# Reordering the last piece's second products, moving half of a gate, and a tile for one weight sum, in a two-layer backbone on one core

## The chip, the core and the metric

The kernel runs on one core of a Trainium2 chip. Its engines are named as in the profile: PE is TensorE (matrix products), PEld its weight loads, DVE is VectorE, ACT is ScalarE, POOL is GpSimd, SP is SyncE, whose queue issues the DMAs. The metric is the device time of one execution in microseconds (us). Before the change it is 2649.41 us, the median of 3 runs (2645.65 to 2652.79).

## What is computed

Two layers work on 512 latent and 128 context tokens of width 1024 in fp32. Each layer is a gated feed-forward block, a token mixer, and a second feed-forward block, so there are four feed-forward blocks in all. The change touches these alone:

```
def swiglu(h, wi, wo):                    # wi: 1024 x 5632, wo: 2816 x 1024
    a, b = jnp.split(h @ wi, 2, axis=-1)
    return (jax.nn.silu(a) * b) @ wo

def trunk_layer(x, mod, ...):
    h = mod_norm(x, norm_g[0], mod, 0)
    x = x + 0.5 * mod[..., 2, :] * swiglu(h, ffn1_wi, ffn1_wo)
    ...                                   # token mixing
    h = mod_norm(x, norm_g[2], mod, 2)
    x = x + 0.5 * mod[..., 8, :] * swiglu(h, ffn2_wi, ffn2_wo)
```

## The kernel before

**Number format.** Every operand of a product is cut in two: a high part (a copy rounded to the matmul's format, on ACT, L265 for weights) and a low part (the rest, a subtraction, on POOL L266 for weights and on DVE L816 for the gated activations). A product is three matmuls into one PSUM sum: high weight by high activation (L449), high weight by low activation (L450), low weight by high activation (L451).

**First products.** The 2816 hidden columns are 22 blocks j of 128. For one j the two halves a and b of the gate come from seven products per block (a 2x2 Strassen-Winograd scheme over the two column groups and the two token halves of 320), in the order S2, S5, A22, A11, S1, S6, S7. Each is twelve matmuls at L773. Their operands on the activation side are B11, B22, X4, X3, X1, X6, X7 (in the profile the names B, X, P, Q). Results go into four PSUM banks, C and E in one tile, D and A in another. After each product DVE or ACT takes its bank: ACT b L831 (S2), DVE b L838 (S5), DVE a L856 (A22), ACT a L846 and DVE b L847 (A11, S1, S6), DVE a L842 and the silu at ACT a L843 (S7). The next product into the same tile waits for such a reader: A22 for L831, S1 for L856.

**The weight sums.** S2, S5, S1 use sums of raw weights, formed on DVE at L124: two in-place differences on the raw buffers (`raw<-raw`, S6 and S7) and one sum into a working tile, `sq` for S2 and S1, `acc` for S5. ACT and POOL then read the sum. `pump` does as many of these conversions as slots allow, after each step; they run about one block j ahead of the products.

**The gate.** `finish`, called in step S7, multiplies the silu'd a by b in two halves of 320 tokens: half 0 reads b in SBUF (`b<-a,b`), half 1 reads bank D (`b<-a,ps`), both at L807. Later `end` makes the high part (ACT av L815) and the low part (DVE av L816). This pair is a "piece".

**Second products.** The j are taken in groups of 4, 2, 4, 4, 4, 4. After a group its n pieces are multiplied by the rows of wo: for each of 8 output slices d, for both token halves g, n pieces of three matmuls, 192 matmuls for n = 4 (`down_part`; `down` for the last group, one g after the other, with the next norm woven in). The rule `late` lets the first `ahead` slices d take all pieces but the last, and only then the last piece of those d, since it is ready latest. Then DVE adds the result to x at L663, which frees the PSUM tile; there are four such tiles. In the first two feed-forward blocks to run, some slices are followed by a burst of small matmuls for the modulation parameters (L376), a copy on ACT (L381) and a transpose on PE (L390).

**Order.** Every engine runs its instructions in the order in which the program writes them; nothing reorders them later.

Of the kernel before, what the change touches and what calls it, by code (L numbers as in the profile page):

```python
# [24 lines left out]
KD = D // 128  # L25
# [59 lines left out]
class Kernel:  # L85
# [26 lines left out]
    def ffn_convs(self, f, u0):  # L112
# [3 lines left out]
        out = []  # L116
# [11 lines left out]
        for j in first:  # L128
            b = ab(j)[1]
# [28 lines left out]
        def s1(r):  # L158
            s7(r)
            s6(r)  # L160
            into(self.nb["sq"][:, :512], q(r[0], 0), q(r[1], 1))

        j0, ud = 0, u0 + 2 * NFF
        for name, j in ((name, j) for j in first for name in ("S1", "S7", "S6")):
# [8 lines left out]
        for gi, gn in enumerate(FFG):  # L173
            for j in range(max(j0, FIRST), j0 + gn):
                a, b = ab(j)
                conv("S2", j, (a, b), lambda r: self.nb["sq"][:, :512], s2)
                conv("S5", j, (a, b), lambda r: self.nb["acc"][:, :512], s5)
                conv("A22", j, (a, b), lambda r: q(r[1], 1))
                conv("A11", j, (a, b), lambda r: q(r[0], 0))
                conv("S1", j, (a, b), lambda r: self.nb["sq"][:, :512], s1)  # L180
                conv("S6", j, (a, b), lambda r: q(r[1], 0), frees=(b,))
                conv("S7", j, (a,), lambda r: q(r[0], 1), frees=(a,))
            for i in range(gn * KD // 8):
                for h in range(2):
                    conv("D", (gi, 2 * i + h), (ud,), lambda r, h=h: q(r[0], h), frees=(ud,) if h else ())
                ud += 1
            j0 += gn
# [256 lines left out]
        return self.modv[l][:, 8 * s + d, cond : cond + 1]  # L444


    def mm3(self, out, w, x, start, stop):
        mm = self.nc.tensor.matmul
        mm(out, w[0], x[0], start=start, stop=False)  # L449
        mm(out, w[0], x[1], start=False, stop=False)  # L450
        mm(out, w[1], x[0], start=False, stop=stop)  # L451

    def rsqrt(self, v, y, a):

# [224 lines left out]
    @staticmethod  # L679
    def late(n, ahead):  # L680


        out = [(d, range(n - 1)) for d in range(ahead)] + [(d, (n - 1,)) for d in range(ahead)]
        return out + [(d, range(n)) for d in range(ahead, KD)]

    def down(self, l, s, pieces, nxt, get, free, ahead, rest=None):

# [5 lines left out]
            self.wcap = 8  # L693
        for g in (1, 0):
            pss = {}
            for d, ks in self.late(n, ahead) if g else [(d, range(n)) for d in range(KD)]:
                self.now += 1
                w = get(d)
                if d not in pss:
                    pss[d] = self.psum()  # L700
                ps = pss[d]
                for k in ks:
                    self.mm3(self.part(ps, g), w(k), pieces[k](g), k == 0, k == n - 1)
                if ks[-1] != n - 1:
                    continue
                if g == d == 0:
                    self.ada_rest()
# [33 lines left out]
    def down_part(self, l, s, pieces, get, free=None, ds=range(KD), ahead=0):  # L741
        n = len(pieces)
        pss = {}
        for d, ks in self.late(n, ahead) if ahead else [(d, range(n)) for d in ds]:
            self.now += 2
            w = get(d)
            if d not in pss:
                pss[d] = self.psum()
            ps = pss[d]
            for g in (1, 0):  # L750
                for k in ks:
                    self.mm3(self.part(ps, g), w(k), pieces[k](g), k == 0, k == n - 1)
            if ks[-1] != n - 1:
                continue
            if free:
                free(d)
            m = 512 - self.geo.n[0]
            flat = ps[:].rearrange("p a b -> p (a b)")[:, m : m + NT]
            self.x_add(l, s, d, flat, ((0, NLAT, 0), (NLAT, NT, 1)), 0)
            self.ada_rest()  # L760
            if free:
                self.pump()
                if d in ADA_AT or (l, 8 * s + KD - 1) not in self.modset:
                    self.ada_tick()
# [14 lines left out]
    def ffn(self, l, s, gate, nxt):  # L779
# [28 lines left out]

        def finish(p, pair):

            gated(p, 0)
            gated(p, 1)
            hi, lo = pair
            b = p["b"]
            ends.append(lambda: nc.scalar.activation(hi, b, AF.Copy))  # L815
            ends.append(lambda: tt(lo, b, hi.bitcast(F32), op=sub))  # L816
# [170 lines left out]
        for gi, gn in enumerate(FFG):  # L987
            pairs = first() if gi == 0 else None
            for j in range(FIRST if gi == 0 else j0, j0 + gn):
                p = new(j)  # L990
                if s and j == NFF - 2:
                    self.ada_stop = True
                banks(p, "CE")
                banks(p, "DA")
                step(p, "S2")
                end(1)
                step(p, "S5")
                end()
                step(p, "A22")
                self.ada_tick()  # L1000
                step(p, "A11")
                step(p, "S1")
                if l == s == 0:
                    self.ada_tick()
                step(p, "S6")
                if pairs is None:
                    pairs = av(gn)
                step(p, "S7", lambda: finish(p, pairs[j - j0]))
# [12 lines left out]
                    self.block_free((f, "D", (gi, d // per)))  # L1021

            if gi < len(FFG) - 1:
                self.down_part(l, gate, pieces, get, free, ahead=2 if n == 4 else 3)
            else:
                if s == 0:
                    self.less_raws((3,))
                else:
# [4 lines left out]
                    self.ada_rest()  # L1033
                    if nxt is not None:
                        self.more_raws((3, 4, 5, 6))
                self.down(l, gate, pieces, nxt, get, free, 2)
                for v in vslots:
                    self.unslot(v)
            j0 += gn
# [962 lines left out]
```

## Time and profile before

| what | value |
|---|---|
| median of 3 runs | 2649.41 us (2645.65 to 2652.79) |
| the profiled execution's own time | 2643.27 us |
| its span, first to last instruction | 2641.2 us |
| PE busy | 2399.8 us, 91% of the span, 17790 matmuls |
| POOL busy | 1551.3 us, 59% |
| DVE busy | 1685.8 us, 64% |
| mean granted TensorE clock | 0.964 of full speed |

A busy PE is not a PE at its peak, as matmuls are pipelined; what counts is how closely one follows another. Idle time of the other engines costs nothing unless PE waits at its end.

### The profile page before, as it was taken

To read this page: it belongs to the slowest core of one execution; us is meant where nothing else is said; L and a number is where in the kernel's file an instruction comes from. 1 tells how busy PE (TensorE), PEld (TensorE's weight loads), DVE (VectorE), ACT (ScalarE), POOL (GpSimd) and SP (SyncE) were. 2 spreads that over 40 slices of the span, in tenths; PEclk is the share of its full clock that TensorE was granted. 3 is DMA by queue.
4 is the path that set the end of the run, shared out by engine and by line. 5 is a ranking of instruction groups with operands and counts; after the bars stand their busy time and mean duration, and the time that the engine had idled before them with its cause. 6 is when DMAs were issued, how large, how long until landed. Compare 5 with 4: busy or idle time off the path is not lost. (4 is left out here: it accounts for less than half of the span.)

```text
span 2641.2 us, 45318 instructions
## 1 busy us (share of the span) xinstructions
PE 2399.8 (91%) x17790; PEld 2330.7 (88%) x17790; DVE 1685.8 (64%) x2902; ACT 1045.4 (40%) x2242; POOL 1551.3 (59%) x1489
## 2 busy tenths in 40 slices
PE   4699999989889899999997999999889898999999
PEld 4699999979889899999987899999889788999999
DVE  5556566567676966555568666556766768566654
ACT  4333233333664533233244332334437644233332
POOL 2655566653366765465556665666434668576553
PEclk7899999989999899999998999999899998999999
DMA  7455422221103224555232221223111133122121
GB/s 269 147 205 208 153 88 80 80 93 55 35 33 104 88 97 174 211 222 198 83 100 71 93 72 65 80 80 123 37 52 43 49 104 112 64 82 87 56 80 48
DMA packets 80484, 272.31 MB, mean 103 GB/s; under 512 B 9233, under 2 KB 15121, under 8 KB 80273
## 3 DMA queue, kind: packets, MB, share of 16 engines
q1 hardware_dynamic: 79408, 269.33, 30.0%
q8 instruction: 140, 2.29, 0.4%
q14 instruction: 72, 0.58, 0.1%
q10 hardware_dynamic: 864, 0.10, 0.0%
HBM read 265.73 MB, written 3.67 MB: 102 GB/s over the span
## 5 line engine op out<-in xcount | busy, mean ns | idle before, releaser
L266 POOL TENSOR_TENSOR wt<-raw,wt 128x512 fp32r<-128x512 f32 (+1 forms) x562 | 875.0, 1575 | 496.9 <-ACT wt L265 493.8
L450 PE MATMUL ps<-av,wt 128*128 128x320 f32 (+2 forms) x1536 | 482.9, 314 | 24.1 <-DVE av L816 24.1
L449 PE MATMUL ps<-av,wt 128*128 128x320 f32 (+2 forms) x1536 | 484.1, 315 | 11.5 <-ACT av L815 11.5
L265 ACT ACTIVATE wt<-raw 128x512 fp32r<-128x512 f32 (+1 forms) x562 | 349.7, 658 | 345.8 <-PE ps L451 120.9
L451 PE MATMUL ps<-av,wt 128*128 128x320 f32 (+2 forms) x1536 | 479.8, 312 | 0.0
L663 DVE SCALAR_TENSOR_TENSOR x<-ps,modv,x 128x512 f32<-128x512 f32 (+3 forms) x496 | 233.3, 513 | 341.9 <-PE ps L451 341.5
L773 PE MATMUL ps<-X,wt 128*128 128x320 f32 x2112 | 355.0, 318 | 48.8 <-DVE a L856 20.3
L773 PEld LDWEIGHTS ps<-X,wt 128*128 128x128 f32 x2112 | 322.9, 193 | 63.1 <-DVE a L856 26.7
L266 POOL TENSOR_TENSOR wt<-sq,wt 128x512 fp32r<-128x512 f32 x144 | 204.3, 1419 | 252.4 <-ACT wt L265 214.4
L773 PE MATMUL ps<-B,wt 128*128 128x320 f32 x2112 | 335.8, 316 | 17.5 <-ACT wt L265 8.0
L773 PEld LDWEIGHTS ps<-B,wt 128*128 128x128 f32 x2112 | 323.2, 193 | 18.7 <-ACT wt L265 8.2
L450 PEld LDWEIGHTS ps<-av,wt 128*128 128x128 f32 x1536 | 294.0, 191 | 30.4 <-DVE av L816 30.3
L773 PE MATMUL ps<-P,wt 128*128 128x320 f32 x1760 | 295.2, 316 | 18.1 <-DVE a L856 11.2
L449 PEld LDWEIGHTS ps<-av,wt 128*128 128x128 f32 x1536 | 293.9, 191 | 15.2 <-ACT av L815 12.5
L451 PEld LDWEIGHTS ps<-av,wt 128*128 128x128 f32 x1536 | 294.0, 191 | 0.0
L773 PEld LDWEIGHTS ps<-P,wt 128*128 128x128 f32 x1760 | 270.3, 192 | 24.9 <-issue 15.2
L847 DVE TENSOR_TENSOR b<-ps,b 128x320 f32<-128x320 f32 x240 | 117.4, 490 | 197.0 <-PE ps L773 135.7
L773 PE MATMUL ps<-Q,wt 128*128 128x320 f32 x1408 | 237.2, 311 | 4.8 <-DVE b L847 4.8
L773 PEld LDWEIGHTS ps<-Q,wt 128*128 128x128 f32 x1408 | 215.6, 190 | 6.0 <-DVE b L847 5.6
L124 DVE TENSOR_TENSOR raw<-raw 128x512 f32<-128x512 f32 x163 | 185.2, 1170 | 8.9 <-DMA raw<-in_w 6.6
L124 DVE TENSOR_TENSOR sq<-raw 128x512 f32<-128x512 f32 x125 | 160.1, 1281 | 29.7 <-POOL wt L266 25.1
L265 ACT ACTIVATE wt<-sq 128x512 fp32r<-128x512 f32 x144 | 90.9, 631 | 221.7 <-DVE sq L124 137.0
(269 smaller groups left out, 3948.4 us busy)
## 6 DMA issues: line engine op xcount, KB each, us to landing
raw<-in_w SPq DMA_DIRECT2D x311, 512.0 KB, 3.6
ada<-in_adat SPq DMA_DIRECT2D x40, 1024.0 KB, 7.5
ada<-in_adat SPq DMA_DIRECT2D x64, 512.0 KB, 6.5
scraw<-in_w SPq DMA_DIRECT2D x33, 512.0 KB, 4.0
x<-in_xt SPq DMA_DIRECT2D x2, 1280.0 KB, 7.8
out_yt<-x SPq DMA_DIRECT2D x16, 160.0 KB, 1.8
dft<-in_dft SPq DMA_DIRECT2D x4, 512.0 KB, 4.1
kqv<-in_inv SPq DMA_DIRECT2D x4, 336.0 KB, 3.9
```

Of the source, the lines that this page charges most:

```text
L124: eng.tensor_tensor(o, x, y, op=op)
L265: nc.scalar.activation(hi, src, AF.Copy)
L266: nc.gpsimd.tensor_tensor(lo, src, hi.bitcast(F32), op=ALU.subtract)
L449: mm(out, w[0], x[0], start=start, stop=False)
L450: mm(out, w[0], x[1], start=False, stop=False)
L451: mm(out, w[1], x[0], start=False, stop=stop)
L663: self.nc.vector.scalar_tensor_tensor(out=self.x[:, d, c0:c1], in0=ps[:, c0 - o : c1 - o], scalar=self.mod(l, s, d, cond), in1=self.x[:, d ...
L773: mm(out, w[:, k * 128 : k * 128 + 128], v[:, k * 320 : k * 320 + 320], start=start and i == k == 0, stop=i == 2 and k == 3, skip_group_ch ...
L847: tt(p["b"][:, half[0]], bank, p["b"][:, half[0]], op=sub if p["neg"] else add)
```

## The change

Three edits. (1) `mm3` can issue only the high-activation matmuls of a product (part 0) or only the low-activation one (part 1). `late` then takes, for the first `ahead` slices, the last piece's high parts for all of them and after that its low parts for all of them; `ahead` is 3 everywhere, where it was 2 for groups of four and in `down`. (2) Half 0 of the gate is issued in step S6 rather than in step S7 (for the first four j it stays). (3) S1's sum goes to the tile `t` instead of `sq`.

```
-            into(self.nb["sq"][:, :512], q(r[0], 0), q(r[1], 1))
+            into(self.nb["t"][:, :512], q(r[0], 0), q(r[1], 1))
...
-                conv("S1", j, (a, b), lambda r: self.nb["sq"][:, :512], s1)
+                conv("S1", j, (a, b), lambda r: self.nb["t"][:, :512], s1)
...
-    def mm3(self, out, w, x, start, stop):
+    def mm3(self, out, w, x, start, stop, part=None):
+
         mm = self.nc.tensor.matmul
-        mm(out, w[0], x[0], start=start, stop=False)
-        mm(out, w[0], x[1], start=False, stop=False)
-        mm(out, w[1], x[0], start=False, stop=stop)
+        if part != 1:
+            mm(out, w[0], x[0], start=start, stop=False)
+        if part != 0:
+            mm(out, w[0], x[1], start=False, stop=part == 1 and stop)
+        if part != 1:
+            mm(out, w[1], x[0], start=False, stop=part is None and stop)
...
-        out = [(d, range(n - 1)) for d in range(ahead)] + [(d, (n - 1,)) for d in range(ahead)]
-        return out + [(d, range(n)) for d in range(ahead, KD)]
+        out = [(d, range(n - 1), None, False) for d in range(ahead)]
+        out += [(d, (n - 1,), i, i == 1) for i in range(2) for d in range(ahead)]
+        return out + [(d, range(n), None, True) for d in range(ahead, KD)]
...
-                if ks[-1] != n - 1:
+                if not all_d:
                     continue
...
-            gated(p, 0)
+            if p["early"]:
+                gated(p, 0)
             gated(p, 1)
...
-                step(p, "S6")
+                step(p, "S6", lambda: gated(p, 0))
...
-                self.down_part(l, gate, pieces, get, free, ahead=2 if n == 4 else 3)
+                self.down_part(l, gate, pieces, get, free, ahead=3)
...
-                self.down(l, gate, pieces, nxt, get, free, 2)
+                self.down(l, gate, pieces, nxt, get, free, 3)
```

The order of instructions on ACT, POOL and SP stays the same; on DVE half 0 of the gate moves, on PE the second products do. Three places show it.

PE, second products of the third group in the third feed-forward block, before. The `ps` numbers are output slices (15634 is d = 0, 15653 is d = 1), av_15231 is the last piece.

```order
L449 MATMUL ps_15653<-av_15231,wt_15446 128x320
L450 MATMUL ps_15653<-av_15231,wt_15446 128x320
L451 MATMUL ps_15653<-av_15231,wt_15446 128x320
L449 MATMUL ps_15653<-av_15231,wt_15446 128x320
L450 MATMUL ps_15653<-av_15231,wt_15446 128x320
L451 MATMUL ps_15653<-av_15231,wt_15446 128x320
L449 MATMUL ps_15695<-av_15229,wt_15479 128x320
```

The same place after the change, where L451, L453 and L455 stand for L449, L450 and L451, av_15232 is the last piece and ps_15672 is d = 2.

```order
L451 MATMUL ps_15653<-av_15232,wt_15446 128x320
L455 MATMUL ps_15653<-av_15232,wt_15446 128x320
L451 MATMUL ps_15672<-av_15232,wt_15480 128x320
L455 MATMUL ps_15672<-av_15232,wt_15480 128x320
L451 MATMUL ps_15672<-av_15232,wt_15480 128x320
L455 MATMUL ps_15672<-av_15232,wt_15480 128x320
L453 MATMUL ps_15634<-av_15232,wt_15446 128x320 x2
L453 MATMUL ps_15653<-av_15232,wt_15446 128x320 x2
L453 MATMUL ps_15672<-av_15232,wt_15480 128x320 x2
L451 MATMUL ps_15722<-av_15230,wt_15480 128x320
```

The low part of the last piece was the 38th matmul of the group's second products (36 before it that use other pieces, one high part); it is now the 67th, behind 54 of other pieces and 12 high parts. Slices 0, 1 and 2 are now complete within six matmuls of each other.

DVE, step S5 to step A11 of a group's first j, before; `sq` is first S1's sum and then the next j's S2 sum.

```order
L124 TENSOR_TENSOR sq<-raw 128x512 [waits Pool_49]
L838 TENSOR_TENSOR b<-b,ps 128x320 [waits PE_49,Activation_49]
L124 TENSOR_TENSOR sq<-raw 128x512 [waits DMAHW0_49,Pool_49]
L856 TENSOR_TENSOR a<-ps,b 128x320 [waits DVE_49,PE_49]
L847 TENSOR_TENSOR b<-ps,b 128x320 [waits DVE_49,Activation_49]
```

The same after the change:

```order
L124 TENSOR_TENSOR t<-raw 128x512 [waits Pool_49]
L844 TENSOR_TENSOR b<-b,ps 128x320 [waits PE_49,Activation_49]
L124 TENSOR_TENSOR sq<-raw 128x512 [waits DMAHW0_49,Pool_49]
L862 TENSOR_TENSOR a<-ps,b 128x320 [waits DVE_49,PE_49]
L853 TENSOR_TENSOR b<-ps,b 128x320 [waits DVE_49,Activation_49]
```

The order is the same, but the second sum no longer overwrites what POOL is about to read; its wait for POOL is now for the previous S2 sum.

DVE, steps S6 and S7 of the same j, before:

```order
L847 TENSOR_TENSOR b<-ps,b 128x320 [waits DVE_49,PE_49]
L124 TENSOR_TENSOR raw<-raw 128x512 x2
L124 TENSOR_TENSOR sq<-raw 128x512 [waits Pool_49]
L842 TENSOR_TENSOR a<-a,ps 128x320 [waits PE_49]
L807 TENSOR_TENSOR b<-a,b 128x320 [waits DVE_49]
L807 TENSOR_TENSOR b<-a,ps 128x320 [waits Activation_49]
```

And after:

```order
L853 TENSOR_TENSOR b<-ps,b 128x320 [waits DVE_49,PE_49]
L812 TENSOR_TENSOR b<-a,b 128x320 [waits DVE_49]
L124 TENSOR_TENSOR raw<-raw 128x512 x2
L124 TENSOR_TENSOR t<-raw 128x512 [waits Pool_49]
L848 TENSOR_TENSOR a<-a,ps 128x320 [waits PE_49]
L812 TENSOR_TENSOR b<-a,ps 128x320 [waits Activation_49]
```

Half 0 of the gate now stands ahead of the three weight sums and of L842 (L848 after the change). In the other j of a group no weight sums lie in between, and it only changes places with L842.

## Rows read from the trace of the kernel before

**Rows 1.** Waits, all engines: who waited for whom, us in total, times, longest.
```profile
DVE x L663 <- PE ps L451: 341.5, 196, 6.3
...
DVE sq L124 <- POOL wt L266: 26.8, 16, 1.7
```

**Rows 2.** Waits of PE alone, same columns.
```profile
PE ps L773 <- DVE a L856: 31.6, 30, 2.6
PE ps L450 <- DVE av L816: 24.1, 24, 1.9
...
PE ps L773 <- ACT b L831: 11.4, 16, 1.3
...
PE ps L773 <- POOL wt L266: 5.1, 4, 2.1
```

**Rows 3.** Timeline, second products: start, length, instruction, [idle before <-releaser].
```profile
1672.00 0.31 PE L449 MATMUL ps<-av,wt 128*128 128x320 f32 x1
...
1677.65 0.81 DVE L816 TENSOR_TENSOR av<-b,av 128x640 fp32r<-128x640 f32 x1
...
1678.52 0.41 PE L450 MATMUL ps<-av,wt 128*128 128x320 f32 x1 [0.93 <-DVE av L816]
```

**Rows 4.** Timeline, PE, the other kinds of groups.
```profile
937.49 0.42 PE L449 MATMUL ps<-av,wt 128*128 128x320 f32 x1 [2.99 <-ACT av L815]
...
999.65 0.42 PE L450 MATMUL ps<-av,wt 128*128 128x320 f32 x1 [1.24 <-DVE av L816]
...
1350.14 0.42 PE L449 MATMUL ps<-av,wt 128*128 128x320 f32 x1 [1.57 <-ACT av L815]
1351.02 0.47 PE L450 MATMUL ps<-av,wt 128*128 128x320 f32 x1 [0.46 <-DVE av L816]
...
1840.62 0.45 PE L450 MATMUL ps<-av,wt 128*128 128x384 f32 x1 [1.84 <-DVE av L816]
```

**Rows 5.** Windows: us, busy of PE, PEld, DVE, ACT, POOL, PEclk, DMA share, GB/s.
```profile
1350.30:1354.30 4.00, 3.54 (x14) 3.31 (x15) 2.02 (x5) 0.95 (x2) 2.25 (x2) 0.62 0.24 52
1355.00:1357.00 2.00, 2.00 (x16) 2.00 (x15) 0.68 (x2) 0.47 (x1) 0.31 (x1) 1.00 1.01 410
```

**Rows 6.** Timeline, first j of a group, products A22, A11 and S1.
```profile
1704.88 1.92 PE L773 MATMUL ps<-X,wt 128*128 128x320 f32 x12
...
1706.64 1.92 PE L773 MATMUL ps<-P,wt 128*128 128x320 f32 x12
...
1707.44 1.76 DVE L124 TENSOR_TENSOR sq<-raw 128x512 f32<-128x512 f32 x1 [1.68 <-POOL wt L266]
...
1709.12 0.48 DVE L856 TENSOR_TENSOR a<-ps,b 128x320 f32<-128x320 f32 x1
...
1709.65 2.03 PE L773 MATMUL ps<-X,wt 128*128 128x320 f32 x12 [1.10 <-DVE a L856]
```

**Rows 7.** Timeline, same j, S6 to the next j's A22.
```profile
1712.01 1.28 POOL L266 TENSOR_TENSOR wt<-acc,wt 128x512 fp32r<-128x512 f32 x1
...
1713.48 0.49 DVE L847 TENSOR_TENSOR b<-ps,b 128x320 f32<-128x320 f32 x1 [1.27 <-PE ps L773]
...
1714.24 3.19 POOL L266 TENSOR_TENSOR wt<-raw,wt 128x512 fp32r<-128x512 f32 x2 [0.95 <-ACT wt L265]
...
1717.90 0.48 DVE L842 TENSOR_TENSOR a<-a,ps 128x320 f32<-128x320 f32 x1
...
1719.25 2.02 PE L773 MATMUL ps<-X,wt 128*128 128x320 f32 x12 [0.53 <-ACT b L831]
```

**Rows 8.** Line L807: ns min/median/max, first and last start, forms.
```profile
L807 DVE TENSOR_TENSOR b<-a,b x88: 477/485/1589, 112.4 to 2609.4; 128x320 f32<-128x320 f32 x88
L807 DVE TENSOR_TENSOR b<-a,ps x72: 472/487/490, 191.9 to 2610.0; 128x320 f32<-128x320 f32 x72
```

**Rows 9.** Timeline, a modulation burst among second products.
```profile
1083.14 1.96 PE L376 MATMUL ada<-ada,scP 128*32 128x128 f32 x64
...
1085.27 0.27 ACT L381 COPY arow<-ada 128x128 f32<-128x128 f32 x1 [0.87 <-PE ada L376]
```

More of the change, by code (lines that the diff above doesn't have):

```diff
@@ L695, in down @@
             pss = {}
-            for d, ks in self.late(n, ahead) if g else [(d, range(n)) for d in range(KD)]:
+            for d, ks, part, all_d in self.late(n, ahead if g else 0):
                 self.now += 1
@@ L702, in down @@
                 for k in ks:
-                    self.mm3(self.part(ps, g), w(k), pieces[k](g), k == 0, k == n - 1)
-                if ks[-1] != n - 1:
+                    self.mm3(self.part(ps, g), w(k), pieces[k](g), k == 0, k == n - 1, part)
+                if not all_d:
                     continue
@@ L743, in down_part @@
         pss = {}
-        for d, ks in self.late(n, ahead) if ahead else [(d, range(n)) for d in ds]:
+        for d, ks, part, all_d in self.late(n, ahead) if ahead else [(d, range(n), None, True) for d in ds]:
             self.now += 2
@@ L751, in down_part @@
                 for k in ks:
-                    self.mm3(self.part(ps, g), w(k), pieces[k](g), k == 0, k == n - 1)
-            if ks[-1] != n - 1:
+                    self.mm3(self.part(ps, g), w(k), pieces[k](g), k == 0, k == n - 1, part)
+            if not all_d:
                 continue
```

## The prediction, made before the run

> **What bounds the kernel now.** I read the waits of all engines first, then those of PE, then the timeline around each kind of wait. DVE waits 341.5 us in 196 places for the second products alone [rows 1], so in these stretches the other engines run after PE and not the reverse. The reader should see that PE's own idle time in the steady part of the feed-forward blocks is short and regular, and that two rows hold most of it: 24.1 us for the low part of a piece and 31.6 us for DVE a L856 [rows 2]. A third, 11.4 us in 16 waits, is for ACT b L831 [rows 2]. Whatever leaves PE's row without being given back at the next wait leaves the time.
>
> Twelve matmuls of 320 columns follow each other in 1706.64 - 1704.88 = 1.76 us, so one costs 0.147 us [rows 6]. A wait of PE costs its idle time plus about 0.1 us, because the first matmul behind it takes 0.41 us instead of 0.31 [rows 3].
>
> **Edit 1, the order of the last piece.** The second products begin at 1672.00, the low part (DVE av L816) is written by 1677.65 + 0.81 = 1678.46, which is 6.5 us later, and PE stood 0.93 us before the low matmul [rows 3]. Now 54 + 12 = 66 matmuls come first, 66 x 0.147 = 9.7 us. The low part is 3.2 us early and the wait goes whole.
> - Groups 3 to 5 of each of the four blocks (12 places like this one): 12 x (0.93 + 0.1) = 12.4 us.
> - The group of two (4 places): `ahead` was 3 already, and 18 + 12 = 30 matmuls (4.4 us) now come before the low part, where 18 + 1 (2.8 us) did. The 1.6 us more covers the wait of 1.24 us [rows 4], with little to spare: 4 x 1.34 = 5.4 us.
> - The last group before a mixer (2 places, matmuls of 384 columns): 27 + 6 = 33 before the low part, where 18 + 1 were. Even at 0.147 us each 14 more are 2.1 us, against a wait of 1.84 us [rows 4]: 2 x 1.9 = 3.8 us.
> - The last group of the second block: PE waits 1.57 us for the high part and 0.46 us for the low one [rows 4]. Nine matmuls more ahead of the high part cover 1.3 us of the 1.57, the six high ones cover the rest of the low part. So about 1.7 us go. Behind these two idle times the granted clock is 0.62 for 4.0 us, a mixture of 1.2 and 2.4 GHz, and 1.00 just after [rows 5]; at full clock the same matmuls would need (1 - 0.62) x 4.0 = 1.5 us less. With an idle time of some 0.3 us instead of 2 I expect full clock: 3.1 us in all, 1.7 if the clock falls all the same.
> - The first group of each block gains nothing. There PE waits 2.99 us for the high part of the third piece, not of the last [rows 4], and the third slice's work on that piece comes behind the same wait.
>
> Sum 24.7 us. What the edit costs: slices 0 to 2 now complete together, at matmuls 68, 70 and 72 where they ended at 42, 48 and 72. Their weight slots and PSUM tiles come free up to 3 us later. Slice 4 takes the tile of slice 0, 24 matmuls (3.5 us) after it ended, and L663 needs about 1 us, so I cost this at nothing; the cover is that conversions run a whole j ahead. One thing is not covered. In 7 groups of the first two blocks a modulation burst follows slice 1 and its transpose follows slice 2. There were 6 or 24 matmuls between burst and transpose, now there are two (0.3 us). ACT begins its copy 1085.27 - 1083.14 - 1.96 = 0.17 us behind the burst and takes 0.27 [rows 9]. PE then waits a few tenths: 7 x 0.4 = 2.8 us, between 1.4 (0.2 each, the copy alone) and 4.9 (0.7, the copy behind one other ACT instruction).
>
> **Edit 3, the tile for S1's sum.** In the first j of a group the next j's S2 sum waits 1.68 us for POOL to read S1's sum from the same tile, and runs until 1709.2; DVE a L856 stands behind it, and PE's S1 waits 1.10 us for that [rows 6]. All 16 such waits together are 26.8 us [rows 1]. With its own tile the sum can run at 1707.44 - 1.68 = 1705.76, while POOL reads the other one or before. L856 then follows A22 directly, and S1 starts without a wait. The 1.10 us stand in 12 first j (they make 13.2 of the 31.6 us [rows 2]): 12 x 1.2 = 14.4 us at that point. In the other 4 a modulation burst on PE covers the wait already, and nothing goes.
>
> **Edit 2, half 0 of the gate.** Where it stood it ran beside the silu on ACT and cost PE nothing. Its new place in a first j is worse. From L847 at 1713.48 DVE forms three weight sums, taking turns with POOL's two subtractions, and L842 comes only at 1717.90; silu and the copy L831 follow, and the next A22 waits 0.53 us for it [rows 7]. Half 0 now goes ahead of these sums. `b<-a,b` reads two SBUF operands and takes 477 ns at best, 1589 at worst, while `b<-a,ps`, with one of them in PSUM, never leaves 472 to 490 [rows 8]. So it can be held up by POOL; the price is 0.4 us, or up to 0.4 + 1.3 = 1.7 us when it first waits out a subtraction of 1.28 us [rows 7].
>
> The Trainium skill, SBUF — State Buffer, section Who interferes with whom, says that a DVE instruction with two SBUF inputs and a GpSimd instruction that reads SBUF exclude each other for the whole instruction. The two lines of L807 agree. By that rule alone half 0 would lose a full subtraction whenever POOL is busy at its new place, which is the second rival below.
>
> Edits 2 and 3 together, in the 12 first j: L847 of S6 comes 1.2 us earlier, near 1712.3. But POOL has the same work in that stretch and starts its subtraction of `acc` perhaps 0.3 us earlier, so it holds until about 1713.0. Half 0 ends near 1713.4, then come two subtractions and three sums in turn as before: L842 came 4.4 us after the start of L847, some 4.0 of it for these. L842 lands at 1717.4 to 1717.7 instead of 1717.90. So of the 1.2 us won at S1 all but some 0.4 is lost again at the next A22: 12 x 0.4 = 4.8 us. Bounds: 12 x 1.2 = 14.4 if half 0 slips in ahead of POOL and hides, and 12 x (1.2 - 1.7) = -6.0. In the 4 first j without a return, half 0 only costs: 4 x 0.65 = 2.6 us, between 1.6 and 6.8. In the other 56 j with a moved half it stands, but for one sum in four of them, in idle time such as the 1.27 us before L847 [rows 7], and I take nothing. Waiting out a subtraction there, 1.7 us, would delay L842 by 1.7 - 1.27 = 0.4 us.
>
> **Sum.** 24.7 + 4.8 - 2.6 - 2.8 = 24.1 us. The profiled execution took 2643.27 us, so 2619.2 us by its own time. It was 6.1 us below the median of the runs shown; against that median, 2649.41, the forecast is 2625 us.
>
> **Rivals.**
> - *Edit 3's gain stays whole.* Half 0 hides beside POOL and the A22 wait shrinks with the rest: 24.7 + 14.4 - 1.4 = 37.7 us, 2612 us. For it: half 0's best time is 0.48. Against: L842 is set by sums and subtractions in turn, and POOL's share of them doesn't shrink.
> - *POOL eats it.* Half 0 waits out a subtraction in every first j: 24.7 - 6.0 - 6.8 - 2.8 = 9.1 us, 2640 us. For it: the 1589 ns; POOL's L266 runs at 1712.01, just where half 0 comes. Against: L842 would have to land 0.5 us later than before although its chain starts 1.2 us earlier.
> - *The next wait takes edit 1's gain.* If the first j's chain kept its hour, the gain of 12.4 us would return as a longer wait there, leaving about 12 us less the bursts and gate, some 7: 2643 us, no change that can be told. Against: that chain begins at the last slice's result, behind 192 matmuls, and DVE waits there for PE.
> - *Slower: the later slots starve the next group.* Slots 0 and 1 come free at matmul 70 instead of 48, 22 x 0.147 less the wait saved = 2.2 us later. If the converted weights were just in time, each of 20 groups would lose this: 44 - 24 = 20 us more, 2669 us. It decides once the lead of the conversions is under 2.2 us. Against: PE waits for POOL's subtraction in four places only, 5.1 us in all [rows 2], and the lead is one j, over 12 us.
>
> **How the numbers follow.** Forecast (24 us, with its own range 14 to 33) 0.60; gain whole 0.15; POOL eats it 0.16; given back 0.06; slower 0.03. The low end is the first rival, 2612; the high end lies by the second, 2639; outside remain the last two and the ends of the others, about 0.17. A difference of 0.3% (8 us, limits 2641.5 and 2657.4) is about what can be told here. Faster by more: all of the forecast, of the first rival and most of the second, 0.90. Within: 0.07. Slower: 0.03.
>
> **What would show it.** In the new profile PE's row for DVE av L816 should fall from 24.1 us to some 4, all of it in first groups; waits of 1.10 for L856 should be gone, those of 0.53 for L831 should have grown to about 1.3, and small waits of the transpose behind a burst should appear. The stretch behind the second block's last group should stay at clock 1.00. DVE's wait of the S2 sum for POOL should vanish. I am wrong on edit 1 if the waits return as waits for the high part or for L663, on edit 2 if L831's row doesn't grow, and on the whole if PE waits for ACT or POOL weights early in a group.

## The result, and the profile after

The changed kernel takes 2612.95 us (median of 4 runs, 2611.36 to 2618.17), the kernel before beside it 2647.53 us. The ratio is 0.9884, with a 95% interval of 0.9866 to 0.9902: 31 us less by the ratio, 34.6 by the two medians. Forecast were 24, with a range of 14 to 33. Run a second time, on another chip, it gave 0.9886 (0.9872 to 0.9899), 30 us. The first profiled execution was one of the longer ones: 2618.17 us with a span of 2616.4, 24.8 us less than the span before.

Busy times from the page:

```profile
PE 2392.8 (91%) x17790; PEld 2331.4 (89%) x17790; DVE 1684.9 (64%) x2902; ACT 1043.4 (40%) x2242; POOL 1548.5 (59%) x1489
```

The engines do nearly the same work as before; what went is idle time of PE. The waits of PE, same columns as [rows 2] (L853 is L847 of before, L862 is L856, L837 is L831, L821/L822 are L815/L816, L812 is L807, L848 is L842):

```profile
PE ada L376 <- DMA ada<-in_adat: 25.3, 9, 14.0
PE ps L778 <- ACT b L837: 22.1, 16, 1.7
PE ps L778 <- DVE a L862: 19.1, 17, 5.4
...
PE ps L451 <- ACT av L821: 8.4, 3, 3.0
...
PE ps L778 <- POOL wt L266: 5.7, 4, 2.1
...
PE ada L390 <- ACT arow L381: 3.4, 5, 1.7
PE ps L453 <- DVE av L822: 3.4, 4, 1.1
```

The low part fell from 24.1 us in 24 places to 3.4 in 4, all in first groups. DVE a L862 fell from 31.6 to 19.1, and ACT b L837 rose from 11.4 to 22.1 in the same 16 places. These are the three movements that the forecast named. A fourth was named too: DVE's wait of the S2 sum for POOL, 26.8 us in [rows 1], is gone from the list. Now the timeline of one group of the third block (start, length, instruction), the second products first, then the first j of the next group, the same places as [rows 3, 6, 7]:

```profile
1576.88 0.31 PE L451 MATMUL ps<-av,wt 128*128 128x320 f32 x1
...
1582.76 0.81 DVE L822 TENSOR_TENSOR av<-b,av 128x640 fp32r<-128x640 f32 x1
...
1586.56 1.04 PE L453 MATMUL ps<-av,wt 128*128 128x320 f32 x6
...
1610.52 0.49 DVE L862 TENSOR_TENSOR a<-ps,b 128x320 f32<-128x320 f32 x1 [0.46 <-PE ps L778]
...
1612.08 1.92 PE L778 MATMUL ps<-X,wt 128*128 128x320 f32 x12
...
1615.39 1.30 POOL L266 TENSOR_TENSOR wt<-acc,wt 128x512 fp32r<-128x512 f32 x1
...
1615.80 0.49 DVE L853 TENSOR_TENSOR b<-ps,b 128x320 f32<-128x320 f32 x1 [1.12 <-PE ps L778]
1616.33 0.71 DVE L812 TENSOR_TENSOR b<-a,b 128x320 f32<-128x320 f32 x1
...
1619.71 1.33 PE L778 MATMUL ps<-B,wt 128*128 128x320 f32 x8
...
1620.97 0.47 DVE L848 TENSOR_TENSOR a<-a,ps 128x320 f32<-128x320 f32 x1
...
1622.31 2.02 PE L778 MATMUL ps<-X,wt 128*128 128x320 f32 x12 [1.27 <-ACT b L837]
1624.17 1.92 PE L778 MATMUL ps<-P,wt 128*128 128x320 f32 x12
```

The low matmuls start 9.7 us after the products begin, as worked out, and the low part has been ready since 1583.57. S1 at 1612.08 has no wait, since L862 now waits for PE and not PE for it. Half 0 (L812) stands behind L853 and lasts 0.71 us, and L848 comes 5.17 us after L853, where it came 4.42 after [rows 7]. PE pays for that at 1622.31.

The last three rows of PE show what a wait costs in full. The eight matmuls from 1619.71 would be done at 1619.71 + 8 x 0.147 = 1620.88, so the next starts 1.43 us late, not 1.27; and its product takes 1624.17 - 1622.31 = 1.86 us instead of 1.76. Together 1.53 us, or 0.26 more than the bracket says. The window of the group (us, busy of PE, PEld, DVE, ACT, POOL, PEclk, DMA share, GB/s) and two behind the second block's last group, beside [rows 5]:

```profile
1542.47:1622.31 79.84, 77.97 (x528) 77.44 (x528) 49.67 (x73) 28.30 (x53) 51.80 (x36) 1.00 0.26 80
...
1342.00:1344.00 2.00, 1.89 (x13) 1.60 (x12) 0.92 (x2) 0.54 (x1) 2.00 (x2) 1.00 0.29 117
1344.00:1346.00 2.00, 2.00 (x16) 2.00 (x15) 1.80 (x6) 1.12 (x3) 0.80 (x2) 1.00 0.16 37
```

The 528 matmuls of a group need 77.45 us (528 x 1.76 / 12, by [rows 6]). To this come two waits, 1.27 for b L837 and 0.60 for a L862 in the third j, each with 0.26 around it: 79.84. Before, four waits (0.93, 1.10, 0.53, 0.60) made 77.45 + 3.16 + 4 x 0.26 = 81.65, the distance of two such waits at 1637.60 and 1719.25. The clock behind the second block's last group is 1.00. L812 by form (ns min/median/max, first and last start), beside [rows 8]:

```profile
L812 DVE TENSOR_TENSOR b<-a,b x88: 479/841/1657, 112.4 to 2583.7; 128x320 f32<-128x320 f32 x88
L812 DVE TENSOR_TENSOR b<-a,ps x72: 486/487/490, 193.8 to 2585.9; 128x320 f32<-128x320 f32 x72
```

The median of half 0 rose from 485 to 841 ns, and half 1, with one operand in PSUM, did not move.

### The profile page after: what moved, and what is told of

Its sections match the earlier page's. It is cut to its first block, busy times and chain, and to the rows that moved or that the text cites. A ratio compares the mean times of both kernels' runs of the same rounds, so it can differ in the third digit from the quotient of the medians.

```text
span 2616.4 us, 45388 instructions
## 1 busy us (share of the span) xinstructions
PE 2392.8 (91%) x17790; PEld 2331.4 (89%) x17790; DVE 1684.9 (64%) x2902; ACT 1043.4 (40%) x2242; POOL 1548.5 (59%) x1489
## 5 line engine op out<-in xcount | busy, mean ns | idle before, releaser
L266 POOL TENSOR_TENSOR wt<-raw,wt 128x512 fp32r<-128x512 f32 (+1 forms) x562 | 871.0, 1567 | 445.9 <-ACT wt L265 442.7
L451 PE MATMUL ps<-av,wt 128*128 128x320 f32 (+2 forms) x1536 | 481.3, 314 | 8.5 <-ACT av L821 8.4
L455 PE MATMUL ps<-av,wt 128*128 128x320 f32 (+2 forms) x1536 | 477.4, 312 | 0.0
L453 PE MATMUL ps<-av,wt 128*128 128x320 f32 (+2 forms) x1536 | 464.3, 313 | 3.4 <-DVE av L822 3.4
L778 PE MATMUL ps<-X,wt 128*128 128x320 f32 x2112 | 351.0, 316 | 48.1 <-ACT b L837 22.1
L451 PEld LDWEIGHTS ps<-av,wt 128*128 128x128 f32 x1536 | 293.4, 191 | 10.9 <-ACT av L821 9.6
L453 PEld LDWEIGHTS ps<-av,wt 128*128 128x128 f32 x1536 | 289.0, 191 | 6.1 <-DVE av L822 4.4
L455 PEld LDWEIGHTS ps<-av,wt 128*128 128x128 f32 x1536 | 293.2, 191 | 0.0
L778 PEld LDWEIGHTS ps<-P,wt 128*128 128x128 f32 x1760 | 271.0, 193 | 24.8 <-issue 16.4
L853 DVE TENSOR_TENSOR b<-ps,b 128x320 f32<-128x320 f32 x240 | 117.4, 489 | 212.3 <-PE ps L778 124.7
L266 POOL TENSOR_TENSOR wt<-t,wt 128x512 fp32r<-128x512 f32 x72 | 95.2, 1322 | 222.3 <-ACT wt L265 174.7
L124 DVE TENSOR_TENSOR raw<-raw 128x512 f32<-128x512 f32 x163 | 194.8, 1228 | 9.0 <-DMA raw<-in_w 6.8
L266 POOL TENSOR_TENSOR wt<-sq,wt 128x512 fp32r<-128x512 f32 x72 | 110.5, 1535 | 72.2 <-ACT wt L265 72.2
L266 POOL TENSOR_TENSOR wt<-acc,wt 128x512 fp32r<-128x512 f32 x72 | 95.5, 1326 | 70.3 <-ACT wt L265 70.3
```

The costliest lines, as they stand in the source:

```text
L124: eng.tensor_tensor(o, x, y, op=op)
L266: nc.gpsimd.tensor_tensor(lo, src, hi.bitcast(F32), op=ALU.subtract)
L453: mm(out, w[0], x[1], start=False, stop=part == 1 and stop)
L455: mm(out, w[1], x[0], start=False, stop=part is None and stop)
L778: mm(out, w[:, k * 128 : k * 128 + 128], v[:, k * 320 : k * 320 + 320], start=start and i == k == 0, stop=i == 2 and k == 3, skip_group_ch ...
L853: tt(p["b"][:, half[0]], bank, p["b"][:, half[0]], op=sub if p["neg"] else add)
```

## The experiments

Since the group repeats exactly, its length (from one wait for b L837 to the next, in groups of four of blocks 1, 3 and 4) tells the variants apart to some 0.05 us, much finer than the timed ratio:

| kernel | ratio to before, interval | a steady group, us | its waits of PE |
|---|---|---|---|
| before | 1 | 81.65 | 0.93, 1.10, 0.53, 0.60 |
| edit 1 | 0.9899 (0.9886 to 0.9912) | 80.44 | 1.10, 0.53, 0.60 |
| edits 1 and 3 | 0.9862 (0.9848 to 0.9876) | 79.45 | 0.88, 0.60 |
| the same again | 0.9851 (0.9837 to 0.9864) | 79.45 | 0.89, 0.60 |
| edits 1 and 2 | 0.9939 (0.9927 to 0.9951) | 80.99 | 1.10, 1.05, 0.60 |
| edits 2 and 3 | 1.0006 (0.9998 to 1.0015) | 81.27 | 1.17, 1.27, 0.60 |
| all three (changed) | 0.9884 (0.9866 to 0.9902) | 79.85 | 1.27, 0.60 |
| all three again | 0.9886 (0.9872 to 0.9899) | 79.85 | 1.28, 0.60 |

**Edit 1 alone.**

```
-            if p["early"]:
+            if True:
                 gated(p, 0)
...
-                step(p, "S6", lambda: gated(p, 0))
+                step(p, "S6")
...
-            into(self.nb["t"][:, :512], q(r[0], 0), q(r[1], 1))
+            into(self.nb["sq"][:, :512], q(r[0], 0), q(r[1], 1))
...
-                conv("S1", j, (a, b), lambda r: self.nb["t"][:, :512], s1)
+                conv("S1", j, (a, b), lambda r: self.nb["sq"][:, :512], s1)
```

> The kernel before with edit 1 alone (order of the last piece). Theory A: each wait of PE costs its idle time and a further 0.1 to 0.26 us around it, and nothing is handed on. So 12 x 1.19 for the 0.93 us waits, 4 x 1.5 for the groups of two, 2 x 2.1 before the mixers, 3.1 behind the second block's last group, less 2.8 for the bursts: 25 us less than before, ratio 0.9906. The waits of 1.10 us for DVE a L862 (L856 before) and of 0.53 us for ACT b L837 (L831 before) stay as they were. Rival (the next wait takes the gain): the chain of the first j keeps its hour, the waits for a L862 grow from 1.10 to about 2.2, and some 12 us are left, ratio 0.9955.

Measured 0.9899, 26.7 us; expected were 25. Timeline of PE, first j of a group:

```profile
1613.26 2.02 PE L778 MATMUL ps<-X,wt 128*128 128x320 f32 x12 [1.09 <-DVE a L862]
...
1622.85 2.02 PE L778 MATMUL ps<-X,wt 128*128 128x320 f32 x12 [0.53 <-ACT b L837]
```

Both later waits have their old lengths, so nothing of the 0.93 is handed on. The rival falls.

**Edits 1 and 3.**

```
-            if p["early"]:
+            if True:
                 gated(p, 0)
...
-                step(p, "S6", lambda: gated(p, 0))
+                step(p, "S6")
```

> The changed kernel with half 0 of the gate back in finish (edits 1 and 3). Theory A: half 0 stands in DVE's chain to L848 and costs all of its time there (L853 to L848 took 5.17 us with it, 4.42 in the kernel before), so without it the wait for ACT b L837 returns to 0.53 us (1.26 in the four places with a burst), the waits of 1.10 stay gone, and the time is 12 x 1.36 less than edit 1 alone: 41 us below before, 10 us below the changed kernel, ratio to before 0.9845. Rival B: the sums in turn with POOL set when L848 comes, and half 0 only fills a gap between them: the wait for b L837 stays at 1.2 to 1.3 us, and the time is that of the changed kernel within 2 us, ratio 0.9884.

Measured 0.9862, between the two. Timeline, S6 to the next j's wait:

```profile
1537.92 1.31 POOL L266 TENSOR_TENSOR wt<-acc,wt 128x512 fp32r<-128x512 f32 x1
...
1538.32 0.49 DVE L853 TENSOR_TENSOR b<-ps,b 128x320 f32<-128x320 f32 x1 [1.12 <-PE ps L778]
1538.73 2.75 DVE L124 TENSOR_TENSOR raw<-raw 128x512 f32<-128x512 f32 x2
1541.41 1.78 DVE L124 TENSOR_TENSOR t<-raw 128x512 f32<-128x512 f32 x1
1543.12 0.47 DVE L848 TENSOR_TENSOR a<-a,ps 128x320 f32<-128x320 f32 x1
...
1544.46 2.02 PE L778 MATMUL ps<-X,wt 128*128 128x320 f32 x12 [0.90 <-ACT b L837]
```

L848 comes 4.80 us after L853: 4.42 before, 5.17 with half 0. Both theories were half right. Of the 1.36 us won at S1 (1.10 and 0.26) POOL takes back 0.37 at once, because its subtraction of `acc` (to 1539.23) now overlaps the first two sums. They take 2.75 us. In the kernel before they took 2.38, as that subtraction was done at 1712.01 + 1.28 = 1713.29 [rows 7], before they began:

```profile
1713.89 2.38 DVE L124 TENSOR_TENSOR raw<-raw 128x512 f32<-128x512 f32 x2
```

Half 0 takes 0.4 more. The tile alone is worth 80.44 - 79.45 = 0.99 us per group, half 0 costs 79.85 - 79.45 = 0.40.

**Edits 1 and 2.**

```
-            into(self.nb["t"][:, :512], q(r[0], 0), q(r[1], 1))
+            into(self.nb["sq"][:, :512], q(r[0], 0), q(r[1], 1))
...
-                conv("S1", j, (a, b), lambda r: self.nb["t"][:, :512], s1)
+                conv("S1", j, (a, b), lambda r: self.nb["sq"][:, :512], s1)
```

> The changed kernel with S1's sum back in the tile sq (edits 1 and 2). Theory A: the waits of 1.10 us for DVE a L862 are back in 12 places, and half 0 adds its 0.75 us to the wait for ACT b L837 all the same (1.27 in 12 places, 1.66 in four): 25 - 12 x 0.75 - 4 x 0.41 = 14 us below before, ratio 0.9946. Rival B (half 0 fills a gap): the wait for b L837 stays near 0.53, the time is that of edit 1 alone, 25 us below before, ratio 0.9906.

Measured 0.9939, 16 us below before. The wait for b L837 is 1.05 here, so half 0 costs 0.52 us against the old tile (0.75 expected), 1.67 in the four others as expected. It does not fill a gap.

**Edits 2 and 3, without edit 1.**

```
-        out += [(d, (n - 1,), i, i == 1) for i in range(2) for d in range(ahead)]
+        out += [(d, (n - 1,), None, True) for d in range(ahead)]
...
-                self.down_part(l, gate, pieces, get, free, ahead=3)
+                self.down_part(l, gate, pieces, get, free, ahead=2 if n == 4 else 3)
...
-                self.down(l, gate, pieces, nxt, get, free, 3)
+                self.down(l, gate, pieces, nxt, get, free, 2)
```

> The kernel before with edits 2 and 3 and without edit 1. Theory A: the parts add up. The low part's waits of 0.93 stay, 1.10 for a L862 (with 0.26 around it) goes in 12 places, the wait for b L837 grows from 0.53 to 1.27 there and from 1.26 to 1.66 in four: 12 x 0.62 - 4 x 0.41 = 6 us below before, ratio 0.9978. Rival C (the gains depend on each other, for instance because edit 1 lets the first j begin at another hour of POOL's work): edits 2 and 3 alone give nothing or lose, ratio 1.000 or above, and b L837 stands at another value than 1.27.

Measured 1.0006: no gain, where theory A had 6 us. In the first j all is as expected (1.27). What A missed lies in the last j of the group:

```profile
1675.88 1.29 POOL L266 TENSOR_TENSOR wt<-acc,wt 128x512 fp32r<-128x512 f32 x1
...
1675.92 1.60 DVE L812 TENSOR_TENSOR b<-a,b 128x320 f32<-128x320 f32 x1
1677.44 0.48 DVE L848 TENSOR_TENSOR a<-a,ps 128x320 f32<-128x320 f32 x1
...
1683.76 0.42 PE L453 MATMUL ps<-av,wt 128*128 128x320 f32 x1 [1.21 <-DVE av L822]
```

Half 0 begins just behind POOL's subtraction, lasts 1.60 us, and everything down to the low part is 0.24 us later; the low part's wait grows from 0.93 to about 1.17 (1.21 in this row). Of the 0.62 us per group 0.38 is left, 12 x 0.38 - 4 x 0.41 = 3 us. These are lost again before the two mixers, and by the same 0.2 us: the low part's wait there grew from 1.84 [rows 4] and 1.86 to 2.05 us, and the granted clock behind it fell. The second mixer's wait, then the windows behind it here and in the kernel before (columns as in [rows 5]):

```profile
1845.21 0.44 PE L453 MATMUL ps<-av,wt 128*128 128x384 f32 x1 [2.05 <-DVE av L822]
...
1845.20:1851.20 6.00, 5.99 (x25) 6.00 (x26) 2.23 (x6) 1.43 (x3) 1.00 (x1) 0.72 0.77 226
...
1840.60:1846.60 6.00, 5.98 (x34) 5.98 (x35) 2.75 (x8) 1.58 (x3) 2.02 (x2) 1.00 0.77 248
```

From this low matmul to PE's next stop of 5.2 us it is 25.41 us here (1845.21 to 1870.62) and 23.87 before (1840.62 to 1864.49), 1.54 more; at the first mixer it is 25.40 and 23.86, again at 0.72 and 1.00. With the longer waits that is 2 x (1.54 + 0.2) = 3.5 us, so the rows add up to about half a microsecond more than before, which the interval of the ratio allows. This profiled execution lost a further 1.7 us around the first mixer (500.39 to 1034.17 before is 533.78 us, here 537.19); why was not tried. The gains do depend on each other, but not in the way of rival C: edit 1 is the cover under which half 0 costs nothing in a last j.

**Count or split.** Two kernels with half of edit 1 each, the rest as changed.

```
-        out += [(d, (n - 1,), i, i == 1) for i in range(2) for d in range(ahead)]
+        out += [(d, (n - 1,), None, True) for d in range(ahead)]
```

> The changed kernel with three slices started early, but the last piece's high and low parts of each slice together again (edit 1 by its count alone). Theory A (what counts is how many matmuls stand before the low part, 0.147 us each): in groups 3 to 5 there are 55 before it (8.1 us) and the low part is ready 6.5 to 6.7 us after the products begin, so the waits there stay gone. In the groups of two nothing changes from the kernel before, and 1.24 us stand again (4 x 1.5); before the mixers 28 stand before it, and some 0.75 of the 2.05 us stay (2 x 1.0); behind the second block's last group 0.46 stays. Together some 8 us more than the changed kernel, 2621 us where that takes 2613, ratio to before 0.991. Rival (the split is what gives): the waits of 0.93 to 1.17 us are back in 12 places, 12 x 1.4 + 8 = 25 us more, ratio 0.998.

```
-                self.down_part(l, gate, pieces, get, free, ahead=3)
+                self.down_part(l, gate, pieces, get, free, ahead=2 if n == 4 else 3)
...
-                self.down(l, gate, pieces, nxt, get, free, 3)
+                self.down(l, gate, pieces, nxt, get, free, 2)
```

> The changed kernel with the last piece split, but two slices started early in groups of four and before the mixers, as before the change (edit 1 by its split alone). Theory A: 36 + 8 = 44 matmuls (6.46 us) stand before the low part, which is ready 6.70 us after the products begin (0.24 us later with half 0 at its new place): waits of 0.2 to 0.3 us, with the refill 0.5, in 12 places. Before the mixers 1.5 of 2.05 us stay (2 x 1.75), behind the second block's last group the wait of 1.57 us for the high part stays, with the half clock behind it 2.6 us. Together some 12 us more than the changed kernel, ratio to before 0.993. Rival (the third slice was not needed): the time is the changed kernel's, 0.9884.

Three slices unsplit: 0.9893 (0.9878 to 0.9908), steady group 79.84, as changed. The waits that stay, before a mixer, in a group of two, and behind the second block's last group:

```profile
535.82 0.44 PE L453 MATMUL ps<-av,wt 128*128 128x384 f32 x1 [0.62 <-DVE av L822]
...
998.66 0.42 PE L453 MATMUL ps<-av,wt 128*128 128x320 f32 x1 [1.22 <-DVE av L822]
...
1346.99 0.41 PE L453 MATMUL ps<-av,wt 128*128 128x320 f32 x1 [0.49 <-DVE av L822]
```

Two slices split: 0.9911 (0.9898 to 0.9924), steady group 80.24, that is 0.18 + 0.26 us of the low part's wait left. The waits behind the second block's last group, in a group of four, and before a mixer:

```profile
1339.28 0.42 PE L451 MATMUL ps<-av,wt 128*128 128x320 f32 x1 [1.42 <-ACT av L821]
...
1660.64 0.85 PE L453 MATMUL ps<-av,wt 128*128 128x320 f32 x4 [0.18 <-DVE av L822]
...
1820.03 0.62 PE L453 MATMUL ps<-av,wt 128*128 128x384 f32 x2 [1.53 <-DVE av L822]
```

All six waits are within 0.15 us of what was expected. So in these rows the number of matmuls ahead of the part that comes late accounts for what is left of the wait, and the split is one way to raise it. Both times came out lower than expected. With two slices the half clock behind the second block's last group, counted in the 2.6 us, did not come (clock 1.00). With three, the waits left make some 8 us and the ratio shows 2; its four runs lie between 2614.91 and 2624.73 us, and what became of the other 6 is open. In groups 3 to 5 the third slice alone does it; the split is what covers the groups of two.

**The sums later.** In front of L848 stand the three sums. This kernel issues them behind S7 in the first j:

```
-                step(p, "S6", lambda: gated(p, 0))
+                step(p, "S6", None, 0 if gi and j == j0 else 99)
```

(half 0 in finish again)

> Edits 1 and 3, half 0 in finish, and in the first j of each group but the first the three weight sums that followed S6 are issued after S7's own work instead. Theory A: these sums in front of L848 are all that makes PE wait for ACT b L837. With the sums behind it, L848 starts when S7 ends, as in the other j, and the waits of 0.88 us (12 places) and 1.27 us (4) go: 12 x 1.14 + 4 x 1.53 = 20 us less than edits 1 and 3 alone, some 57 us below before, ratio 0.9785. Rival D (the sums are needed where they are): the three sums and POOL's work on them end later and the next j's sum of S2 or DVE a L862 is late, the waits for a L862 grow from 0.60 to 1.5 us or more, and at most 5 us go, ratio 0.985.

Measured 0.9906 (0.9893 to 0.9920): some 12 us worse than edits 1 and 3. The waits for b L837 are all gone. Two new ones stand in their place, and that of the third j grew from 0.60 to 0.70:

```profile
1540.85 1.78 DVE L124 TENSOR_TENSOR t<-raw 128x512 f32<-128x512 f32 x1
1542.55 0.47 DVE L844 TENSOR_TENSOR b<-b,ps 128x320 f32<-128x320 f32 x1
...
1543.08 2.02 PE L778 MATMUL ps<-P,wt 128*128 128x320 f32 x12 [0.73 <-DVE b L844]
1545.81 2.02 PE L778 MATMUL ps<-X,wt 128*128 128x320 f32 x12 [0.70 <-DVE a L862]
1559.20 1.01 PE L778 MATMUL ps<-X,wt 128*128 128x320 f32 x5 [0.70 <-DVE a L862]
```

The sums now stand in front of L844, and the work of DVE and POOL behind them slides into the next j. In kind this is rival D, and it was worse than D said: 80.48 us per group, though no single wait reached 1.5 us. The three waits, each with 0.26, make 80.36; the other 0.12 stand in no row of a wait.

**The low part later as well.** The same, with `end()` (L822) behind A22's L862 in every j:

```
                 step(p, "S5")
-                end()
                 step(p, "A22")
+                end()
```

> The kernel with the later sums, and with the low part of a piece (DVE av L822) written after A22's DVE a L862 instead of before it. Theory A: the 0.60 us waits for a L862 in the second j of a group come from L822 alone, which POOL holds up to 1.4 us there; they go in 12 places: 12 x 0.86 = 10 us less than the run with the later sums alone, ratio to before 0.975. Rival: L822 then delays the sum for S1 or the next b L853 by as much, the wait moves to PE's next product (ACT wt L265 or DVE b L853 rows grow), and nothing is gained, ratio 0.9785.

Measured 0.9897 (0.9884 to 0.9911), steady group 79.61. Two waits are left (0.74 for L844, 0.64 for DVE b L853): in the second j of a group the wait moved on, as the rival said, in the third it went. These two account for 79.35 us; 0.26 stand in no row of a wait.

**Half 0 in all j but the first,** beside the changed kernel and edits 1 and 3 on one chip:

```
-            if p["early"]:
+            if p["early"] or "first" in p:
...
-                step(p, "S6", lambda: gated(p, 0))
+                step(p, "S6", p.update(first=1) if j == j0 else lambda: gated(p, 0))
```

> The changed kernel once more, beside the next three on one chip. Theory A (the parts add up by their rows: edit 1 alone 26 us, S1's tile 1.0 us per steady group more, half 0 0.38 us per steady group and 0.41 in four others less): some 31 us below before, ratio 0.988, and 6 us above edits 1 and 3 alone.

> Edits 1 and 3 once more. Theory A: half 0 at S6 costs 12 x 0.38 + 4 x 0.41 = 6 us, so 6 us below the changed kernel, ratio to before 0.986. Rival: half 0 costs nothing outside these rows or gives it back elsewhere, and the two kernels come out alike within 3 us.

> The changed kernel with half 0 at S6 in all j but the first of each group, where it is in finish again. Theory A: half 0 costs in the first j alone, elsewhere it stands in idle time or in front of a low part that edit 1 no longer waits for: the wait for ACT b L837 falls from 1.27 to 0.9 us in 12 places and from 1.66 to 1.27 in four, and the time is that of edits 1 and 3, ratio 0.986. Rival: half 0 costs in the other j as well (it ran 1.6 us beside POOL in the last j of a group): the time stays near the changed kernel's, 0.988, though the waits for b L837 fall.

Measured 0.9886, 0.9851 and 0.9865 (0.9851 to 0.9879); medians 2614.47, 2604.90 and 2609.56 us, spans 2611.6, 2605.0 and 2607.4. The first two lie 6.6 us apart by their spans and 9.6 by their medians, 6 were expected. Without half 0 in the first j the group takes 79.46 us, as with edits 1 and 3, though half 0 still lasts 1.57 us in a last j (1572.53). So in a steady group it costs in the first j alone. The 2 to 5 us between this kernel and edits 1 and 3 lie outside these groups and within what runs differ by; whether half 0 costs something in the other groups stays open.

**The better version.** From the two runs on later work only the part that did not come back, L822 behind L862 in the third j, on edits 1 and 3:

```
-                end()
+                end(0 if j == j0 + 2 else 2)
                 step(p, "A22")
+                end()
```

> Edits 1 and 3, half 0 in finish, and in the third j of each group the low part of the piece (DVE av L822) written after A22's DVE a L862 instead of before it. Theory A: PE's wait of 0.60 us for a L862 there comes from L822 alone and goes in 12 places, 12 x 0.86 = 10 us less than edits 1 and 3 alone, ratio to before 0.982. Rival: as with the later sums, the work comes back one product later (a wait of 0.6 us for DVE b L853 in the same j), and the time is that of edits 1 and 3, 0.986.

Measured 0.9827 (0.9813 to 0.9842), 2598.83 us: 45 us below before and 16 below the changed kernel beside it. Against edits 1 and 3 it is 6 us by the medians and 10.4 by the spans (2605.0 and 2594.6), expected were 10. The group takes 78.58 us, 0.87 less (0.86 expected):

```profile
1548.00 0.49 DVE L862 TENSOR_TENSOR a<-ps,b 128x320 f32<-128x320 f32 x1 [0.47 <-PE ps L778]
1548.47 1.40 DVE L822 TENSOR_TENSOR av<-b,av 128x640 fp32r<-128x640 f32 x1
...
1549.56 1.92 PE L778 MATMUL ps<-X,wt 128*128 128x320 f32 x12
1550.23 0.49 DVE L853 TENSOR_TENSOR b<-ps,b 128x320 f32<-128x320 f32 x1 [0.37 <-ACT a L852]
```

L822 is still 1.40 us long beside POOL, but L853 behind it had to wait for ACT anyway.

## Why the forecast held, and where its terms were off

**The wait itself** was mis-sized. I took 0.1 us beside each wait, it is 0.26, as shown above. With that, the 12 places are worth 12 x 1.20 (81.65 to 80.44) instead of 12 x 1.03, the groups of two 4 x 1.50 instead of 4 x 1.34.

**The last group of the second block** came as forecast, a little larger. From its first second product to the end of the first token half, 108 matmuls, the kernel before took 19.96 us (1345.77 to 1365.73), edit 1 alone 16.38 (1337.64 to 1354.02). They need 108 x 1.76 / 12 = 15.84. So before the change 4.12 us were lost there: 1.57 + 0.46 + 2 x 0.26 for the two stops, and 1.57 for the clock, forecast 1.5. Edit 1 alone leaves one stop of 0.26 with 0.26 around it, and the clock stays at 1.00. The gain is 3.6 us, forecast 3.1.

**The bursts** came as forecast too, but the row of waits hides most of them: ACT arow L381 rose from 2.3 to 3.4 us only, all of it in one wait of 1.7. In the other six groups the transpose waits for the copy too, without a bracket in the view:

```profile
1080.76 0.56 PE L453 MATMUL ps<-av,wt 128*128 128x320 f32 x2
1081.01 0.27 ACT L381 COPY arow<-ada 128x128 f32<-128x128 f32 x1 [0.82 <-PE ada L376]
1081.33 0.33 PE L390 MATMUL ada<-ident,arow 128*128 128x128 f32 x1
...
1081.65 0.30 PE L453 MATMUL ps<-av,wt 128*128 128x320 f32 x1
```

From the start of the last matmul ahead of the transpose (1080.76 + 0.56 - 0.31 = 1081.01) to that of the second behind it is 0.64 us; in the kernel before, where the copy was long done, it is 0.40 (1088.50 to 1088.90). So six times about 0.2 us, the low end of the forecast, and 1.1 in the first group of the first block, where the copy stands behind two weight conversions of ACT that wait for a DVE sum: some 2.4 us, forecast 2.8. A term that the forecast lacked is the DMA of the bursts' matrices. PE's waits for in_adat without the first, at the program's start, were 9.3 us before, 11.3 here and 9.6 in the repeat, so it costs between 0.3 and 2 us. That PE reaches the bursts sooner would explain it, but this was not tried.

**Edits 2 and 3 together** had 0.4 us per group, and got 80.44 - 79.85 = 0.60. The reasoning (most of what S1 wins is lost at the next A22, through POOL first and half 0 after it) is what the runs with one of them each showed: 1.36 won, 0.37 lost to POOL, 0.40 to half 0. Half 0's price was put at 0.4 to 1.7 and is the low end. So the first rival falls, since even without half 0 the gain is not whole, and the second, since half 0 overlaps only a part of POOL's subtraction. In the four other first j the cost is 1.67 - 1.26 = 0.41, forecast 0.65.

**"In the other 56 j I take nothing"** was right only under a cover that the step did not name. The idle time of 1.27 us, which stands before L842 in a last j as well, does not hold 1.57 us of half 0 (the forecast had allowed for 0.4 us of delay there, and 0.24 came); what hides the rest in the last j of a group is edit 1, and without it the low part's wait grows by 0.24.

**Given back, starved:** edit 1 alone left both next waits at 1.09 and 0.53, and POOL L266 stands at 5.7 us in four places, as before (5.1). Neither rival happened.

The corrected terms add 12 x 0.17 + 4 x 0.16 + 12 x 0.20 + 4 x 0.24 = 6.0 us to the 24.1: 30.1. The smaller ones (0.5 behind the second block, 0.4 before the mixers by 2 x 2.1 instead of 2 x 1.9, 0.4 less for the bursts) make it 31.4, the DMA takes back 0.3 to 2. Measured were 31 and 30, so the account closes to within a microsecond or two, and no closer. That the median of the first pair, 2612.95 us, stands at the number of the first rival, 2612, is chance: that rival needed the whole gain of edit 3. The first profiled pair shows only 24.8, and most of what is missing lies in one stretch, over the second mixer (1782.03 to 2310.74): 528.71 us there and 524.54 in the repeat of the same kernel. The two executions agree to 0.01 us for the first 78 us of it and part inside the mixer, where the granted clock is 0.91 in the first (1869.0 to 1912.0) and 1.00 in the repeat (1868.4 to 1909.4). What lowered it there is open.

## What to carry to other kernels

Where work repeats, account for one period, as matmuls plus waits plus what each wait costs around it; most variants can then be read from their own trace to 0.1 us, where timed runs blur 3 us. A wait that ends on a second engine is seldom removed by moving the instruction in front of it: ask what that instruction will stand in front of next, and move only what lands ahead of something that waits anyway. And an instruction moved into idle time is free only as long as its longest form, beside POOL's subtraction, fits there. And a slightly longer stop can cost more than its length: look at the granted clock behind it.

## What the runs showed that was not expected

- A stop of PE costs 0.26 us more than its bracket in these rows: 0.16 between the last matmul's slot and the start of the idle time, 0.10 at the restart.
- `b<-a,b` at its new place lasts anything from 0.48 to 1.66 us. In the last j it begins 0.04 us after a POOL subtraction and ends 0.35 us after it (1675.92 + 1.60 against 1675.88 + 1.29). The Trainium skill, SBUF — State Buffer, section Who interferes with whom, calls the ports that DVE shares with GpSimd an exclusive lock, and says of DVE's two-port modes that whichever comes first holds them for its whole instruction; of a DVE instruction with two SBUF inputs it says that it contends. These rows agree, and show the whole subtraction waited out for such an instruction too.
- A small difference in PE's idle time went with a fall of the granted clock. Behind the second block's last group, with 0.49 us alone (three slices unsplit) and with 1.42 us alone (two slices split) it stayed at 1.00; with 1.57 and 0.46 us it was 0.62 [rows 5]. Before the mixers, with 1.84 and 1.86 us it stayed at 1.00, and with 2.05 us it was 0.72 over the next 6 us, in both places (edits 2 and 3).
